# Output product and second norm of a hybrid block written in one fixed order: six token tiles begun, two finished by pairs of w_out's rows

## The chip, the cores and the metric

One core of a Trainium2 chip runs the whole kernel. The metric is the device time of one execution in microseconds. TensorE is the matmul engine, VectorE, ScalarE and GpSimd are the elementwise engines (DVE, ACT and POOL in the rows), and SyncE (SP) issues nearly all DMAs from one queue, in order.

## The reference

One layer: a bidirectional RG-LRU block over 256 context and 1024 latent tokens, then a gated ConvFFN over the latent tokens. D_MODEL is 1024, LRU_WIDTH 1280, FFN_HIDDEN 2816, batch 1, fp32. What matters for the change is the end of the mixer and the norm behind it:

```python
out = lambda y, r: (jax.nn.gelu(y) * r.astype(y.dtype)) @ w_out      # r: both scans, added
x = x + gate1 * out(y_lat, r_lat)                                    # only the latent tokens are kept
h2 = rms_norm(x) * (1.0 + scale2) + shift2                           # second norm, feeds the ConvFFN
u = h2 @ w_up                                                        # then conv 3x3, silu(a) * v, w_down
```

(The last three lines are the layer's wiring in short; rms_norm divides by the root of the mean square of 1024 channels.)

## The kernel before

Every fp32 product is made of three matmuls on a rounded "high" part and the "low" rest: high x high, low x high, high x low (`mm`, line 87). The high part is a cast on ScalarE, the low part a subtraction (`lo_part`, line 84) on VectorE or GpSimd. So each operand of a product costs one cast and one subtraction of its size before TensorE can read it.

The scans run channels on partitions: ten blocks t of 128 channels, each 1280 tokens wide. Block t's result, scan forward plus scan backward times gelu(y), goes to DRAM: blocks 0 to 7 to `rgd`, block 8 to `rgd8`, block 9 to `rgd9`. The output product runs tokens on partitions: eight token tiles i of 128, two halves c of 512 output columns, ten blocks k. For one tile and half that is 30 matmuls of 128x512. The tile's operand is read back from `rgd` as an 8x128 slab (`rgr`), split into `rgh` and `rgl`. In the first half, blocks 8 and 9 come from SBUF (`r8h/l`, `r9h/l`), in the second from DRAM (`rg2`). w_out comes in pairs m of row blocks (2m, 2m+1) for one half: `wo_pair(pool, c, m)` loads 512 KB (`wor`), casts (`woh`) and subtracts (`wol`). There are two raw buffers for these pairs, shared with all other weights (tag `raw`), and five split ones.

The first half is begun while the last block's scans run (lines 638 to 697). `first(i)` does blocks 0 to 7 of tile i into a bank of PSUM; five tiles are begun (five banks of `ps_b`), then block 8 is added to the five, then block 9. This part is written under a manual schedule: TensorE, VectorE, ScalarE and GpSimd execute it in the order of the text. From line 700 on there is no manual schedule; a scheduler orders the instructions from the loop over c and i. It does tiles 5 to 7 of the first half whole, then the second half in banks `ps_d` (two, used in turn). For each tile, `pb` is multiplied by the gate g1 and added to x1 (lines 744 and 745). In the second half x1[i] is then complete, and the norm follows at once: square and sum, Sqrt, reciprocal and a Newton step (`rstd_of`), scale and shift into `xn`, eight transposes on TensorE into `pt` (two banks of `ps_t`), cast and subtraction into `h2h` and `h2l`. The first two up-projection tiles take tokens 0 to 511 before the last tile's norm, and tokens 512 to 1023 after it. The rest of the ConvFFN, the same in both kernels, follows.

Of the kernel before, what the change touches and what calls it, by code (L numbers as in the profile page):

```python
# [19 lines left out]
P = 128  # L20
# [45 lines left out]
def tile_kernel(ctx: ExitStack, tc: tile.TileContext, x, cx, par, mod_b, mod1, mod2, wyx, gw, w_out, w_up, w_down, fw, out):  # L66
# [52 lines left out]
    def rstd_of(n, srcs, junks, between=lambda: None):  # L119
# [7 lines left out]
        return [rs[:, i:i + 1] for i in range(m)]  # L127

# [371 lines left out]
    def rg_part(i, c):  # L500
        gh = op.tile([P, NCH, P], F32R, tag="rgh", name="rgh", bufs=2)
        gl = op.tile([P, NCH, P], F32R, tag="rgl", name="rgl", bufs=2)
        raw = op.tile([P, NCH - 2, P], F32, tag="rgr", name="rgr")
        cols = slice(i * P, (i + 1) * P)
        load(raw, rgd[:, :, cols].rearrange("t p n -> p t n"))
        S.copy(gh[:, :NCH - 2], raw)
        lo_part(V, gl[:, :NCH - 2], raw, gh[:, :NCH - 2])
        if c:
            r2 = op.tile([P, 2, P], F32, tag="rg2", name="rg2", bufs=2)
            for j in range(2):  # L510
                load(r2[:, j], rgd2[j][:, cols])
            S.copy(gh[:, NCH - 2:], r2)
            lo_part(V, gl[:, NCH - 2:], r2, gh[:, NCH - 2:])
        return gh, gl

    def out_mm(pb, c, i, rgs, ks):
        for k in ks:
# [3 lines left out]
            else:  # L521
                gh, gl = (r[:, k] for r in rgs)
# [26 lines left out]
    with tc.manual_schedule(engines={ENG.PE, ENG.DVE, ENG.Activation, ENG.Pool}):  # L549
# [102 lines left out]
        rgs = {0: rg0, 1: rg_load(op0, 1, 3), 2: rg_load(op0, 2, 3)}  # L652
        S.copy(rgs[1][0], rgs[1][2])
# [7 lines left out]
        def first(i):  # L661
            pbs[i] = bank()
            out_mm(pbs[i], 0, i, rgs[i][:2], range(NCH - 2))
# [3 lines left out]
        a_t = [decay(t, d, r_t[d]) for d in range(2)]  # L667
# [15 lines left out]
        lo_part(V, rgs[4][1], rgs[4][2], rgs[4][0])
        first(4)
        lo_part(V, last2[NCH - 2][1], hs8, last2[NCH - 2][0])
        wo_pair(op, 0, 4, V)
        recur(1, a_t[1], r_t[1], b_t[1])
        for i in range(5):
            out_mm(pbs[i], 0, i, None, (NCH - 2,))
# [4 lines left out]
        S.copy(last2[NCH - 1][0], hs)  # L694
        lo_part(V, last2[NCH - 1][1], hs, last2[NCH - 1][0])
        for i in range(5):
            out_mm(pbs[i], 0, i, None, (NCH - 1,))


    ps_x.release()  # L700
    wo_pair(wp, 1, 0)
# [24 lines left out]
    for c in range(2):  # L726
# [9 lines left out]
        for i in range(KD):  # L736
# [9 lines left out]
            if c == 0:  # L746
                continue
# [234 lines left out]
```

## Time and profile before

| | us |
|---|---|
| median of 3 runs | 1267.95 (1265.47 to 1268.74) |
| profiled execution | 1267.6 |
| its span, first to last instruction | 1265.8 |
| TensorE busy, VectorE busy | 1219.2, 1028.0 |
| ScalarE busy, GpSimd busy | 547.3, 398.9 |

The span divides into a head with the modulation, the blocks of the mixer with their scans up to about 389 us, the output product and second norm up to about 550 us, and the ConvFFN from there. A busy TensorE is not one at its peak: matmuls overlap, a 128x512 one is listed with 0.39 us and starts every 0.23 us. In the profile's rows the brackets give the idle time of an engine ahead of an instruction and what ended it.

### The profile page before, as it was taken

Reading aid. Unit: us, or ns where it says so; the run is one execution under the profiler, and the core shown is the slowest. Engines: PE = TensorE matmul, PEld = TensorE weight load, DVE = VectorE, ACT = ScalarE, POOL = GpSimd, SP = SyncE. Lnnn points to the kernel's source line nnn. Section 1 sums busy time; section 2 is a strip of 40 time slices with the busy share of each in tenths; the row PEclk is TensorE's granted clock in tenths of the full one; section 3 lists DMA queues with packets and bytes.
Section 4 is the critical chain, followed back from the end, with each engine's and each line's share of the span. In section 5 each row is a group of like instructions: output and inputs, shape, how many; then the busy total and the mean of one; then the engine's idle time right before and its main releaser. Section 6 shows DMA issues by size and latency. Waiting matters only on the chain.

```text
span 1265.8 us, 14253 instructions
## 1 busy us (share of the span) xinstructions
PE 1219.2 (96%) x5512; PEld 1001.2 (79%) x5512; DVE 1028.0 (81%) x1156; ACT 547.3 (43%) x691; POOL 398.9 (32%) x221
## 2 busy tenths in 40 slices
PE   7879999999999889999999999999999999999996
PEld 6768888888887668788888888888888888888875
DVE  6968999999978758679878777777777778777777
ACT  6468888888888134333212222222222112222244
POOL 4732222222220010252333333333333333334460
PEclk8789999999999999999999999999999999999999
DMA  8522333333325552221111111111111111111003
GB/s 321 179 69 98 125 125 126 125 125 125 109 67 154 199 178 85 67 79 40 49 50 50 51 50 50 50 50 37 41 41 50 50 51 50 50 50 50 17 1 133
DMA packets 55588, 108.21 MB, mean 85 GB/s; under 512 B 4440, under 2 KB 22872, under 8 KB 55520
## 3 DMA queue, kind: packets, MB, share of 16 engines
q1 hardware_dynamic: 55376, 107.04, 25.4%
q8 instruction: 43, 0.70, 0.2%
q10 hardware_dynamic: 144, 0.26, 0.1%
q14 instruction: 25, 0.20, 0.1%
HBM read 97.85 MB, written 9.44 MB: 85 GB/s over the span
## 4 chain that ended last, share of the span: by engine, by line
PE 83%; DVE 9%; ACT 3%; DMA 2%; issue 2%; POOL 1%; SPq 0%; ACTq 0%; DVEq 0%; POOLq 0%
PE u L87 37%; PE pd L87 21%; PE pb L87 14%; PE xp L87 10%; DVE hl L214 2%; DVE acc L803 1%; DVE o L922 1%; DVE md L215 1%; DMA wor<-w_out_dram 1%; DMA ld<-x_dram 1%; DVE rgl L84 1%; DVE x L836 1%; DMA rgr<-rgd 0%; PE pt L763 0%; PE pb L271 0%
## 5 line engine op out<-in xcount | busy, mean ns | idle before, releaser
L803 DVE SCALAR_TENSOR_TENSOR acc<-u,pr,acc 128x945 f32<-128x945 f32 (+2 forms) x352 | 427.1, 1219 | 24.7 <-ACT acc L796 17.3
L87 PE MATMUL u<-h2l,wh 128*128 128x512 f32 x704 | 276.6, 393 | 0.0
L87 PE MATMUL u<-h2h,wh 128*128 128x512 f32 x704 | 276.0, 392 | 0.2 <-ACT h2h L766 0.2
L87 PE MATMUL u<-h2h,wl 128*128 128x512 f32 x704 | 274.3, 390 | 0.0
L84 POOL TENSOR_TENSOR wl<-raw,wh 128x1024 fp32r<-128x1024 f32 x66 | 164.4, 2491 | 270.4 <-ACT wh L151 252.6
L836 DVE TENSOR_TENSOR x<-pd,x 128x512 f32<-128x512 f32 x160 | 109.2, 686 | 125.7 <-PE pd L87 125.7
L87 PEld LDWEIGHTS u<-h2h,wh 128*128 128x128 f32 x704 | 132.3, 188 | 29.9 <-ACT h2h L766 0.5
L87 PEld LDWEIGHTS u<-h2h,wl 128*128 128x128 f32 x704 | 132.7, 188 | 29.0
L87 PEld LDWEIGHTS u<-h2l,wh 128*128 128x128 f32 x704 | 132.6, 188 | 28.9 <-DVE h2l L84 0.4
L87 PE MATMUL pd<-dl,gh 128*128 128x512 f32 x320 | 126.4, 395 | 0.0
L87 PE MATMUL pd<-dh,gh 128*128 128x512 f32 x320 | 125.7, 393 | 0.8 <-ACT dt L833 0.8
L87 PE MATMUL pd<-dh,gl 128*128 128x512 f32 x320 | 124.4, 389 | 0.0
L882 ACT CAST gh<-acc 128x1024 fp32r<-128x1024 f32 x22 | 23.2, 1053 | 223.5 <-DVE acc L879 223.5
L84 POOL TENSOR_TENSOR gl<-acc,gh 128x1024 fp32r<-128x1024 f32 x18 | 43.3, 2408 | 198.8 <-ACT gh L882 198.8
L878 ACT ACTIVATE acc<-acc 128x1024 f32<-128x1024 f32 x22 | 23.3, 1060 | 182.8 <-DVE acc L803 182.8
L151 ACT CAST wh<-raw 128x1024 fp32r<-128x1024 f32 x64 | 67.2, 1050 | 75.7 <-PE u L87 69.9
L87 PE MATMUL xp<-hh,wh 128*128 128x512 f32 (+1 forms) x240 | 85.6, 369 | 2.0 <-ACT hh L224 2.0
L87 PE MATMUL xp<-hl,wh 128*128 128x512 f32 (+1 forms) x240 | 81.3, 364 | 4.0 <-POOL hl L84 4.0
L87 PEld LDWEIGHTS pd<-dh,gh 128*128 128x128 f32 x320 | 60.0, 187 | 14.0 <-ACT dt L833 1.2
L87 PEld LDWEIGHTS pd<-dl,gh 128*128 128x128 f32 x320 | 60.0, 187 | 13.9
L87 PEld LDWEIGHTS pd<-dh,gl 128*128 128x128 f32 x320 | 60.2, 188 | 13.4
L815 POOL TENSOR_TENSOR dr<-dr,g 128x512 f32<-128x512 f32 x40 | 51.5, 1306 | 57.9 <-DMA dr<-w_down_dram 57.9
(205 smaller groups left out, 2229.9 us busy)
## 6 DMA issues: line engine op xcount, KB each, us to landing
raw<-w_up_dram SPq DMA_DIRECT2D x44, 512.0 KB, 3.4
mraw<-mod_dram SPq DMA_DIRECT2D x64, 256.0 KB, 4.1
raw<-wyx_dram SPq DMA_DIRECT2D x20, 512.0 KB, 3.6
dr<-w_down_dram SPq DMA_DIRECT2D x40, 256.0 KB, 4.7
ld<-mod_dram SPq DMA_DIRECT2D x16, 512.0 KB, 5.2
rgr<-rgd SPq DMA_DIRECT2D x16, 512.0 KB, 5.1
rgd<-r SPq DMA_DIRECT2D x10, 512.0 KB, 3.2
wor<-w_out_dram SPq DMA_DIRECT2D x10, 512.0 KB, 4.9
```

Source lines behind the costliest of these rows:

```text
L84: eng.tensor_tensor(lo, src, hi.bitcast(F32), op=ALU.subtract)
L87: T.matmul(o, w, r, start=start, stop=stop)
L151: S.copy(wh, raw)
L214: V.scalar_tensor_tensor(hl[KD - 1][:, :D], mr[k][s], 1.0, row, op0=ALU.mult, op1=ALU.mult, accum_out=md1[:, k, s, v:v + 1])
L215: V.tensor_scalar(md1[:, k, s], md1[:, k, s], mod_b1(k, s), None, op0=ALU.add)
L803: V.scalar_tensor_tensor(o, uv[:, r0 + dy:r1 + dy, c0 + dx:c1 + dx], w(dy, dx), o, op0=ALU.mult, op1=ALU.add)
L815: G.tensor_tensor(raw, raw, g2[:, cs], op=ALU.mult)
L836: V.tensor_tensor(xs, pd, xs, op=ALU.add)
L878: ordered(act(aa, aa, AF.Silu))
L882: S.copy(gh, aa)
L922: V.scalar_tensor_tensor(o, x1[i], rs, fwb, op0=ALU.mult, op1=ALU.mult)
```

## The change

The manual schedule now reaches to the end of the first two up-projection tiles, so the order of the four engines is that of the text (SyncE's is still the scheduler's).

First half: the eight banks of PSUM hold more tiles, since `ps_x` (three banks) is released early. Six tiles are begun with blocks 0 to 7. Loads are issued apart from the splits (`wo_load`, `wo_split`; `rg_load` one or two tiles ahead). The decays of the last block write to the memory of `xh` and `xl` and stand ahead of the previous block's sum. Block 9's split is done in halves of 512 tokens. Tiles 6 and 7 follow together, one pair of w_out's rows after the other, and behind each pair the buffers are refilled with the same pair of the second half. The gate and the add into x1 stand between these passes.

Second half: a tile's slab is loaded and split two tiles ahead (`rg_all`, `rg_split`); a tile's transposes stand two tiles behind its product, those of the last two among the up matmuls. The root is an estimate on ScalarE (Abs_reciprocal_sqrt) and a Newton step, in place of Sqrt, reciprocal and Newton. The low parts of w_out's last pairs and of the first two up weights are all on VectorE.

```diff
+    def rstd_est(ss, nv, rs, src, junk):
+        if src is not None:
+            act(junk, src, AF.Square, accum_out=ss, scale=D ** -0.5)
+        ordered(act(rs, ss, AF.Abs_reciprocal_sqrt, bias=eps))
+        act(nv, ss, AF.Identity, bias=meps, scale=-0.5)
...
+        ps_x.release()
+        ps_f = pool("ps_f", bufs=3, side="right", space=PSUM)
...
-        wo_pair(wp, 0, 2, V)
-        wo_pair(op, 0, 3, V)
+        wo_load(0, 2)
+        wo_load(0, 3)
...
+        lo_part(V, rgs[1][1], rgs[1][2], rgs[1][0])
+        rgs[3] = rg_load(op0, 3, 3)
         recur_scan(1, prev[1][1], prev[3][1])
-        lo_part(V, rgs[1][1], rgs[1][2], rgs[1][0])
+        lo_part(V, rgs[2][1], rgs[2][2], rgs[2][0])
+        rgs[4] = rg_load(op, 4, 2)
+        wo_load(1, 0)
+
+        a_t = [wk.tile([P, NTOK], F32, tag=tag, name="a") for tag in ("xh", "xl")]
+        for d in range(2):
+            decay_a(t, d, r_t[d], a_t[d])
+            decay_b(t, d, r_t[d])
...
+            pbs[i] = ps_f.tile([P, 512], F32, tag="pb", name="pb") if i in (2, 3, 4) else bank()
...
+        first(5)
+        recur_scan(1, a_t[1], b_t[1])
+        for i in range(6):
+            out_mm(pbs[i], 0, i, (NCH - 2,))
...
+        for q in range(2):
+            cols = slice(q * 512, (q + 1) * 512)
+            S.copy(last2[NCH - 1][0][:, cols], hs[:, cols])
+            lo_part(V, last2[NCH - 1][1][:, cols], hs[:, cols], last2[NCH - 1][0][:, cols])
+        for i in range(6):
+            out_mm(pbs[i], 0, i, (NCH - 1,))
...
+        for m in range(5):
+
+            for i in (6, 7):
+                out_mm(pbs[i], 0, i, (2 * m, 2 * m + 1))
+            wo_split(wp if m < 3 else op, 1, m, V)
+            if m < 3:
+                wo_load(1, m + 2)
+            if m == 0:
+                to_gated(4)
...
+            elif m == 1:
+                rg_split(0)
+                rg_all(1)
+                to_x1(4)
+                to_x1(5)
+            elif m == 3:
+                rg_split(1)
+        for i in (6, 7):
+            to_gated(i)
+            to_x1(i)
...
+        cs = slice(512, D)
+        for i in range(KD):
+            if i + 2 < KD:
+                rg_all(i + 2)
+            pbs[i] = ps_d.tile([P, 512], F32, tag="pd", name="pd")
+            out_mm(pbs[i], 1, i, range(2))
+            if i > 1:
+                turn(i - 2)
+                h2_part(i - 2, True)
+            out_mm(pbs[i], 1, i, range(2, NCH))
+            if i > 1:
+                h2_part(i - 2, False)
+            to_gated(i)
+            to_x1(i)
+            if i + 2 < KD:
+                rg_split(i + 2)
+            if i == KD - 1:
+                wu[tiles[1]] = split(raw, V)
+            xns[i] = op1.tile([P, D], F32, tag="xn", name="xn", bufs=2)
+            ss, nv, rs, tm = (stat[:, j, 10 + i:11 + i] for j in range(4))
+            rstd_est(ss, nv, rs, x1[i], xns[i])
+            rstd_step(nv, rs, tm)
...
+        for k in range(3):
+            up_k(0, us[0], 0, k)
+        turn(KD - 2)
...
+        for k in range(KD // 2):
+            up_k(1, us[1], 0, k)
+        turn(KD - 1)
```

`turn(i)` is the eight transposes of tile i, `h2_part` its casts (True) or its subtractions (False), `to_gated` and `to_x1` the gate and the add.

The first place where the order is read is VectorE around the last block's scans. Before (r_3289 is the last block's result, a_3399 its backward scan, rgl the low parts of token tiles, r9rgl that of block 9):

```order
L84 TENSOR_TENSOR wol_3505<-wor_3502,woh_3504 128x1024
L459 SCALAR_TENSOR_TENSOR r_3289<-a_3399,r_3289 128x1280
L84 TENSOR_TENSOR rgl_3589<-rgr_3590,rgh_3588 128x1024
L460 TENSOR_TENSOR b_3307<-b_3307,r_3289 128x1280
L467 SCALAR_TENSOR_TENSOR a_3399<-a_3399,b_3307 128x256
L468 SCALAR_TENSOR_TENSOR a_3399<-a_3399,b_3307 128x1024
L473 TENSOR_TENSOR r_3289<-a_3396,a_3399 128x1024
L477 TENSOR_TENSOR r_3289<-r_3289,gy_3236 128x1024
L84 TENSOR_TENSOR rgl_3629<-rgr_3630,rgh_3628 128x1024
L84 TENSOR_TENSOR r9rgl_3531<-r_3289,r9rgh_3530 128x1024
```

After (a_3361 is that scan, rgl_3489 and rgl_3520 are tiles 6 and 7):

```order
L84 TENSOR_TENSOR rgl_3452<-rgr_3453,rgh_3451 128x1024
L470 SCALAR_TENSOR_TENSOR r_3289<-a_3361,r_3289 128x1280
L471 TENSOR_TENSOR b_3307<-b_3307,r_3289 128x1280
L84 TENSOR_TENSOR r8l_3456<-r_3056,r8h_3455 128x1024
L84 TENSOR_TENSOR wol_3527<-wor_3342,woh_3526 128x1024
L478 SCALAR_TENSOR_TENSOR a_3361<-a_3361,b_3307 128x256
L479 SCALAR_TENSOR_TENSOR a_3361<-a_3361,b_3307 128x1024
L484 TENSOR_TENSOR r_3289<-a_3360,a_3361 128x1024
L488 TENSOR_TENSOR r_3289<-r_3289,gy_3236 128x1024
L84 TENSOR_TENSOR r9rgl_3583<-r_3289,r9rgh_3582 128x512 x2
L84 TENSOR_TENSOR rgl_3489<-rgr_3490,rgh_3488 128x1024
L84 TENSOR_TENSOR rgl_3520<-rgr_3521,rgh_3519 128x1024
```

One tile's subtraction has moved from among the scan's steps to ahead of them, the one between the result and block 9's low part to behind it, and block 9's is two instructions of 512.

The second place is VectorE at the end of the first half. Before (wol are w_out's last pairs, pb_3667 is tile 7 of the first half, pd_3755 tile 0 of the second):

```order
L84 TENSOR_TENSOR wol_3713<-wor_3710,woh_3712 128x1024
L84 TENSOR_TENSOR rgl_3824<-rgr_3825,rgh_3823 128x1024
L744 TENSOR_TENSOR pb_3667<-pb_3667,g1_82 128x512
L84 TENSOR_TENSOR wol_3719<-wor_3716,woh_3718 128x1024
L745 TENSOR_TENSOR x1_7_3570<-pb_3667,x1_7_3570 128x512
L84 TENSOR_TENSOR wol_3725<-wor_3722,woh_3724 128x1024
L84 TENSOR_TENSOR rgl_3824<-rg2_3829,rgh_3823 128x256
L84 TENSOR_TENSOR wol_3731<-wor_3728,woh_3730 128x1024
L744 TENSOR_TENSOR pd_3755<-pd_3755,g1_82 128x512
L745 TENSOR_TENSOR x1_0_3563<-pd_3755,x1_0_3563 128x512
```

After (wol_3749 is the last pair, pb_3643 and pb_3644 are tiles 6 and 7, wl is the first up weight, pd_3791 tile 0 of the second half):

```order
L84 TENSOR_TENSOR wol_3711<-wor_3661,woh_3710 128x1024
L84 TENSOR_TENSOR wol_3729<-wor_3683,woh_3728 128x1024
L84 TENSOR_TENSOR rgl_3690<-rgr_3691,rgh_3689 128x1024
L84 TENSOR_TENSOR rgl_3690<-rg2_3692,rgh_3689 128x256
L84 TENSOR_TENSOR wol_3749<-wor_3714,woh_3748 128x1024
L755 TENSOR_TENSOR pb_3643<-pb_3643,g1_82 128x512
L758 TENSOR_TENSOR x1_6_3620<-pb_3643,x1_6_3620 128x512
L755 TENSOR_TENSOR pb_3644<-pb_3644,g1_82 128x512
L758 TENSOR_TENSOR x1_7_3621<-pb_3644,x1_7_3621 128x512
L84 TENSOR_TENSOR wl_3763<-raw_3760,wh_3762 128x1024
L755 TENSOR_TENSOR pd_3791<-pd_3791,g1_82 128x512
L758 TENSOR_TENSOR x1_0_3614<-pd_3791,x1_0_3614 128x512
```

The last three pairs stood among and behind tile 7's gate and add; now gate and add of tiles 6 and 7 stand behind the last pair, and the first up weight's subtraction stands between them and the second half's first tile.

## Rows read from the trace of the kernel before

**Rows 1.** The page: chain that ended last, shares of the span by engine.

```profile
PE 83%; DVE 9%; ACT 3%; DMA 2%; issue 2%; POOL 1%; SPq 0%; ACTq 0%; DVEq 0%; POOLq 0%
```

**Rows 2.** Windows, 376 to 550 us: length, busy time (x instructions), granted clock, DMA.

```profile
390.00:400.00 10.00, 7.57 (x33) 5.70 (x32) 9.35 (x9) 6.43 (x7) 0.00 (x0) 1.00 0.43 142
...
420.00:430.00 10.00, 5.86 (x21) 4.28 (x20) 8.39 (x7) 2.10 (x2) 0.00 (x0) 0.88 0.50 153
...
460.00:470.00 10.00, 7.64 (x24) 5.17 (x25) 5.03 (x7) 4.16 (x6) 2.39 (x1) 0.83 0.56 174
...
520.00:530.00 10.00, 8.03 (x34) 6.30 (x33) 9.19 (x14) 2.41 (x5) 2.26 (x1) 0.83 0.63 202
```

**Rows 3.** Waits of TensorE, 376 to 600 us: us, times, longest.

```profile
PE pb L87 <- ACT r9rgh L694: 3.4, 1, 3.4
PE pb L87 <- DVE rgl L84: 2.4, 1, 2.4
PE pd L87 <- ACT woh L488: 2.4, 2, 1.9
PE pt L763 <- DVE xn L758: 2.0, 1, 2.0
PE pb L87 <- DVE x L745: 1.4, 1, 1.4
```

**Rows 4.** Timeline, TensorE: start us, us, engine, line, operation, out<-in, xcount.

```profile
389.00 0.40 PE L87 MATMUL pb<-woh,rgh 128*128 128x512 f32 x1
...
398.03 0.40 PE L87 MATMUL pb<-woh,rgh 128*128 128x512 f32 x1
...
419.43 0.39 PE L87 MATMUL pb<-wol,rgh 128*128 128x512 f32 x1
...
427.85 0.80 PE L87 MATMUL pb<-woh,r9rgl 128*128 128x512 f32 x1 [0.77 <-DVE r9rgl L84]
```

**Rows 5.** Chain of waits by time, 378 to 600 us: start, us, what.

```profile
453.15 4.32 DMA wor<-w_out_dram
...
459.82 3.65 DMA wor<-w_out_dram
...
474.74 0.87 PE pt L763 x8
...
539.00 46.80 PE u L87 x204
```

**Rows 6.** Windows, 550 us to the end (columns as in rows 2).

```profile
550.00:600.00 50.00, 50.00 (x221) 41.27 (x221) 47.94 (x43) 16.51 (x16) 16.70 (x9) 1.00 0.18 62
```

**Rows 7.** Lines by form, VectorE, 389 to 530 us: xcount, busy, mean, idle.

```profile
L84 DVE TENSOR_TENSOR rgl<-rgr,rgh 128x1024 fp32r<-128x1024 f32 x15 | 18.3, 1221 | 7.6 <-ACT rgh L506 7.5
...
L84 DVE TENSOR_TENSOR h2l<-pt,h2h 128x512 fp32r<-128x512 f32 x14 | 9.0, 684 | 2.6 <-ACT h2h L766 2.5
...
L744 DVE TENSOR_TENSOR pd<-pd,g 128x512 f32<-128x512 f32 x8 | 5.6, 695 | 2.3 <-PE pd L87 2.2
...
L468 DVE TENSOR_TENSOR_SCAN a<-a,b 128x1024 f32<-128x1024 f32 x2 | 4.7, 2352 | 0.1
```

**Rows 8.** Timeline, ScalarE; in brackets the idle time before, and releaser.

```profile
398.58 1.37 ACT L442 ACTIVATE a<-r,sp 128x1280 f32<-128x1280 f32 x1 [3.52 <-DVE r L473]
...
404.02 1.28 ACT L669 ACT_TABLE_LOAD   x1
405.31 2.44 ACT L669 ACTIVATE r<-r 128x1280 f32<-128x1280 f32 x2
```

**Rows 9.** Waits of VectorE, 376 to 540 us.

```profile
DVE r L459 <- ACT r L669: 2.3, 1, 2.3
```

**Rows 10.** Tile rgr, 370 to 530 us: last line of its answer.

```profile
DMA to landing us min/median/max: 4.2/4.8/5.3
```

**Rows 11.** Lines by form, ScalarE, 389 to 530 us (columns as in rows 7).

```profile
L488 ACT CAST woh<-wor 128x1024 fp32r<-128x1024 f32 x8 | 8.3, 1048 | 7.7 <-DMA wor<-w_out_dram 6.2 <-PE pb L87 1.6
```

**Rows 12.** Tile x, 370 to 470 us: the loads of x1.

```profile
DMA to landing us min/median/max: 10.8/10.8/10.8
```

More of the change, by code (lines that the diff above doesn't have):

```diff
@@ L521, in out_mm @@
             else:
-                gh, gl = (r[:, k] for r in rgs)
+                gh, gl = (r[:, k] for r in rgs[i][:2])
             mm(pb, gh, wh[:, k % 2], k == 0, False)
@@ L693, in tile_kernel @@
         last2[NCH - 1] = [op0.tile([P, LAT], F32R, tag=n, name=f"r9{n}", bufs=3) for n in ("rgh", "rgl")]
[L694 to L701, printed above, removed]
-    opa.release()
-    wk.release()
-    gwp.release()
-    x1p = pool("x1")
-    x1 = [x1p.tile([P, D], F32, name=f"x1_{i}") for i in range(KD)]
-    def weight_up(n):
-        raw = wp.tile([P, KD, P], F32, tag="raw", name="raw", bufs=2)
-        load(raw, w_up[n].rearrange("p (k m) -> p k m", k=KD))
-        return split(raw, G)
@@ new lines, in tile_kernel @@
+        for q in range(2):
[5 more added lines that the diff above has]
+        for i in (6, 7):
+            lo_part(V, rgs[i][1], rgs[i][2], rgs[i][0])
+        opa.release()
+        wk.release()
+        gwp.release()
+        x1p = pool("x1")
+        x1 = [x1p.tile([P, D], F32, name=f"x1_{i}") for i in range(KD)]
@@ new lines, in x1_load, with to_gated, to_x1 @@
+        def x1_load(i):
+            load(x1[i], x[i * P:(i + 1) * P])
+        def to_gated(i):
+            V.tensor_tensor(pbs[i], pbs[i], g1[:, cs], op=ALU.mult)
+        def to_x1(i):
+            V.tensor_tensor(x1[i][:, cs], pbs[i], x1[i][:, cs], op=ALU.add)
+        cs = slice(0, 512)
+        for i in range(4):
+            x1_load(i)
+        rg_all(0)
+        for i in range(4, KD):
+            x1_load(i)
+        for i in range(3):
+            to_gated(i)
+        to_x1(0)
+        to_gated(3)
@@ new lines, in tile_kernel, with up_load, weight_up, up_psum @@
+        for i in (6, 7):
+            to_gated(i)
+            to_x1(i)
+        op0.release()
+        op1 = pool("op1", side="right")
+        tiles = [n for j in range(NF) for n in (j, NF + j)]
+        wu = {}
+        us = {}
+        def up_load(n):
+            raw = wp.tile([P, KD, P], F32, tag="raw", name="raw", bufs=2)
+            load(raw, w_up[n].rearrange("p (k m) -> p k m", k=KD))
+            return raw
+        def weight_up(n):
+            return split(up_load(n), G)
+        def up_psum(pos):
+            return (ps_u2 if pos % 3 == 2 else ps_u).tile([P, LAT], F32, tag="u", name="u")
@@ new lines, in tile_kernel, with turn @@
+        raw = up_load(tiles[1])
+        ps_f.release()
+        ps_b.release()
+        ps_d = pool("ps_d", bufs=2, space=PSUM)
+        ps_u = pool("ps_u", bufs=2, space=PSUM)
+        ps_t = pool("ps_t", bufs=2, side="right", space=PSUM)
+        h2p = pool("h2")
+        h2h = h2p.tile([P, KD, LAT], F32R, name="h2h")
+        h2l = h2p.tile([P, KD, LAT], F32R, name="h2l")
+        xns, pts = {}, {}
+        def turn(i):
+            pts[i] = [ps_t.tile([P, 512], F32, tag="pt", name="pt") for q in range(2)]
+            for k in range(KD):
+                T.transpose(pts[i][k // 4][:, k % 4 * P:(k % 4 + 1) * P], xns[i][:, k * P:(k + 1) * P], ident)
```

172 lines of the change are left out of this document (80 added, 92 removed).

## The prediction

> **What bounds the kernel now.** I read the chain of waits first: TensorE holds 83% of it [rows 1]. So only those stretches can give time where TensorE stands still or runs at a lower clock. The windows show where: 420 to 430 us has a granted clock of 0.88, 460 to 470 and 520 to 530 have 0.83, and 390 to 400 has TensorE busy only 7.57 of 10 us at full clock [rows 2]. All lie in the output product and second norm, which is what is changed. The waits of TensorE name the causes: 3.4 us for the high part of the last channel block (r9), 2.4 for the low part of token tile 1, 2.4 for w_out's high part, 2.0 for the normed tile xn, 1.4 for x1 [rows 3].
>
> How much is lost there in all? The product's matmuls start at 389.00 us. Those from 398.03 to 419.43 are 92 intervals: 0.2326 us each [rows 4]. The work up to the end of the first two up-projection tiles is fixed: 480 product matmuls x 0.2326 = 111.6 us, eight sets of transposes x 0.87 = 7.0, and 96 up matmuls x 0.2294 (46.80 us for 204) = 22.0 [rows 5]: 140.6 us. The last 48 of these start at 539.00 [rows 5] and end at 539.00 + 48 x 0.2294 = 550.0. So 161.0 us pass for 140.6 of work: **20.4 us are lost**, 11.6 of them in the five waits shown, about 10 x (0.12 + 0.17 + 0.17) = 4.6 by the clock, the rest in short gaps. After 550 us TensorE is busy without a break (50.00 of the first 50) [rows 6].
>
> **The change part by part.**
> *First half, tiles 0 to 5.* The wait of 2.4 for tile 1's low part goes: its subtraction now stands ahead of two scans, of which the longer alone takes 2.35 [rows 7], so it ends about 3 us earlier, more than the wait was long; TensorE asks at 389.0 + 25 x 0.2326 = 394.8. Exp no longer takes the memory of the previous block's a tiles, for which it idled 3.52 us [rows 8]; it takes that of xh and xl, which the gate matmuls have left by 389. So Sqrt ends some 3.5 us earlier, and the 2.3 us for which VectorE stood before the last r go [rows 9]. For r9: VectorE did the same five tile subtractions before it; now it is 2.3 us earlier, one subtraction of 1.22 [rows 7] stands behind r9's, and r9 is split into halves (0.6 less). TensorE had the first low part at 427.85 [rows 4]; now 427.8 - 2.3 - 1.2 - 0.6 = 423.7, and 1 to 2 us more where dependent steps have no cover between them: up to 425.6. TensorE has a sixth tile in front: 389.0 + 144 x 0.2326 + 18 x 0.23 = 426.6. The wait is gone with 1.0 to 2.9 us to spare. Tile loads: each needs the buffer of the tile two before it; loads land in 4.2 to 5.3 us [rows 10]. Tile 5's is late next: its buffer is free when tile 3's subtraction ends, about 404.3, and SP has the rgd8 store and the first rg2 read (which waits for that store) ahead of it; issued at 404.8 it lands by 410.1, is cast in 1.05 [rows 11] and is in time for the subtraction at about 411.2.
>
> *Tiles 6 and 7.* Both have free banks and parts, so the wait for x1 goes. 60 matmuls: 430.7 to 444.8 (= 389.0 + 240 x 0.2326, no wait). The two passes share the w_out pair m, and after each pass its buffers are split anew for the second half. This is the place of my first cost. Pair (1,0) can be cast at 433.5 and is subtracted by 435.9; only then may load (1,2) go (two raw buffers), landing after 3.65 to 4.32 us as its like did [rows 5], about 440.2. Behind tile 0's casts and subtractions and two x1 adds VectorE reaches (1,2) at 442.5 and ends at 443.7; load (1,4) goes at 443.8 and lands at 448.1; cast and subtraction: 450.4. TensorE wants its low part at 444.8 + 26 x 0.2326 = 450.9. No wait, but nothing to spare. The eight x1 loads, 10.8 us to landing before [rows 12], are ahead of them in the queue: issued from about 424.4, right behind block 9's store, and done by about 438.
>
> *Second half.* VectorE's queue has gate and add of tiles 6 and 7 behind the subtraction of pair (1,4): 450.4 + 4 x 0.695 = 453.2 [rows 7]. As the program is built, the first pd tile lies in the bank of tile 1, long free, but the second in the bank of tile 7. TensorE reaches the second at 444.8 + 30 x 0.2326 = 451.8 and waits: 453.2 - 451.8 = 1.4, with the handing over **1.5** (bounds: 0.8 if the load lands after 3.65 us, 2.4 if after 5.3). Such a wait (1.9, 2.0) was followed by a mean clock of 0.83 in its 10 us; the one of 2.4 was not [rows 2, 3]. Bounds 0 and 1.7; I take 1.7. Then the first transposes: the normed tile 0 needs gate and add 1.4, square and root about 1.9 (a pass of ScalarE like the cast's 1.05 [rows 11], and small steps), one table load 1.28 [rows 8], Newton about 0.4, xn two passes like the subtractions' 1.22: about 0.3 us later than TensorE asks: 0.3.
>
> From there a tile takes TensorE 30 x 0.2326 + 0.87 = 7.85 us. VectorE has three passes of 1.22, 2 x 0.684 and 2 x 0.695 = 6.4 [rows 7], about 0.9 of small ones, and waits about 0.5 for the root: just inside. The transposes, now two tiles later, ask 9.2 us after the product, xn is there after 6.2: the 2.0 us wait for xn goes. Tile 7's is asked for 36 up matmuls after its product (8.3 + 0.9) and ready after 8. The root itself (two small VectorE instructions fewer per tile) lies beside TensorE: nothing. Up weights on VectorE instead of GpSimd: wl of tile 0 is in the chain above, that of tile 1 falls in the last tile's slack.
>
> A rule speaks against the root's new table. The Trainium skill (ScalarE: Activation LUTs, "What ACT_TABLE_LOAD costs") counts 1.28 us plus a drain of about 1.38 for every switch. The trace here has 1.28, and the next instruction starts at 405.31, 1.29 us after the load began [rows 8]; no drain shows. By the rule the first transposes would wait 1.7, not 0.3 us, and the sum would be 1.4 us higher.
>
> *Sum:* -20.4 + 1.5 + 1.7 + 0.3 = **-16.9 us**. The profiled execution took 1267.6, 0.35 below the median of 1267.95: 1267.6 - 16.9 + 0.35 = **1251.0 us**.
>
> **The rivals.**
> *No new wait* (0.20): loads land early enough or the wait for tile 7's bank is short and leaves the clock. For it: 3.65 is a landing seen. Against: VectorE's order itself puts four instructions behind the last split. -20.4: 1247.5.
> *w_out's loads stay late* (0.22): the second half starts with the waits of before (2.4 for woh, the subtraction, 1.7 of clock: about 4.5) on top of mine, because x1 and tile loads crowd the queue. For it: before, x1 took 10.8 us. Against: here x1 starts earlier. 1255.5; with one wait more, 1259.
> *The up-projection eats it* (0.03): VectorE is busy 47.94 of 50 us from 550 to 600 [rows 6]; if it sets the pace there, TensorE's earlier start becomes a wait. Against: VectorE's start moves with it, and TensorE waits for nothing there. 1268.
> *Slower* (0.04): the tile load as the second half's clock. One raw buffer: load, cast 1.05, subtraction 1.22, then the next load. With 4.8 us to landing [rows 10] that is 7.2, below 7.85. With x1's 10.8 it is 13.2: six tiles x 5.4 = 32 us, less the gain: 1283. It decides from a landing of 5.4, and breaks even at 5.4 + 16.9/6 = 8.2. Against: no x1 load is in flight then.
>
> **How the numbers follow.** My forecast has 0.51, its own range is 1248.5 to 1253.5. The range for 8 in 10 takes in the case without waits and the late loads: 1246.5 to 1259. A measurement here can tell about 0.3%, 3.8 us, from no change: faster means below 1264.1. Faster: 0.51 + 0.20 + 0.22 = 0.93; same 0.03; slower 0.04.
>
> **What would show it.** In the waits of TensorE the rows for r9rgh, rgl, woh, xn and x should be gone or under 0.5 us, and one row pd <- DVE x (the add of tile 7) of 1 to 2 us should be new, near 452 us. The first up matmul should stand near 509, not 522. A clock of 1.00 in every window but the one at 450 to 460. I am wrong if TensorE waits for tiles' parts (rgl) again, if waits for w_out's low parts exceed 2 us, or if the stretch from 389 us to the end of the second up tile is not 142 to 148 us long.

## The result and the profile after

Before 1267.58 us (median of 4 runs), after **1248.53 us** (1246.67 to 1250.26, 4 runs): ratio 0.985, 95% interval 0.983 to 0.987. The forecast was 1251.0.

| | before | after |
|---|---|---|
| profiled execution, us | 1267.6 | 1246.7 |
| its span, us | 1265.8 | 1244.8 |
| first matmul of the product, us | 389.00 | 387.95 |
| **stage**: from there to the end of the second up-projection tile, us | 161.0 | **141.15** |

The span is 21.0 us shorter. 19.9 of them lie in the stage that the change rewrites; 1.05 lie ahead of it, in a part that is the same in both. In some executions that part takes about 10 us more, so rows of different runs stand up to 11.5 us apart, and the experiments are compared by the stage's length rather than by times of day. The stage is worked out as in the prediction: after, the last transposes start at 514.68, 126.73 us after the first product matmul, and 60 up matmuls follow them; for every run below it is that distance plus the same 14.42.

The chain that ended last, by engine, answers to [rows 1]:

```profile
PE 86%; DVE 8%; ACT 3%; DMA 1%; issue 1%; POOL 0%; SPq 0%; ACTq 0%; DVEq 0%
```

The windows, with the columns of [rows 2]:

```profile
390.00:400.00 10.00, 10.00 (x44) 7.95 (x43) 9.93 (x9) 9.89 (x9) 0.00 (x0) 1.00 0.58 185
...
420.00:430.00 10.00, 10.00 (x46) 8.25 (x45) 9.19 (x12) 1.14 (x2) 0.00 (x0) 1.00 0.71 260
...
450.00:460.00 10.00, 9.20 (x40) 7.00 (x39) 8.28 (x12) 4.92 (x8) 0.00 (x0) 1.00 0.66 214
460.00:470.00 10.00, 10.00 (x52) 8.37 (x52) 9.41 (x14) 6.20 (x15) 0.00 (x0) 1.00 0.23 68
```

All waits of TensorE from 376 to 600 us, answering to [rows 3]:

```profile
PE pd L87 <- DVE x L758: 0.8, 1, 0.8
PE pb L87 <- DVE b L449: 0.3, 1, 0.3
```

All five waits of before are gone, TensorE is busy 10.00 of 10 where it had 7.57 and 5.86, and no window from 380 to 550 us has a granted clock under 1.00. (The granted clock is a mean over the window: 1.00 is the higher of the clock's two levels, 2.4 GHz, and 0.83 says that TensorE ran part of the 10 us at the lower one, 1.2 GHz.) The row of 0.3 lies ahead of the product and was there before. The one new wait is the one foretold, for the bank of tile 7, one of the first half's last two tiles. TensorE's timeline at that place:

```profile
450.19 0.39 PE L87 MATMUL pd<-wol,rgh 128*128 128x512 f32 x1
451.38 0.50 PE L87 MATMUL pd<-woh,rgh 128*128 128x512 f32 x1 [0.80 <-DVE x L758]
```

From start to start 1.19 instead of 0.23: 0.96 us lost. VectorE there (start, duration, in brackets the idle time before and its releaser):

```profile
445.37 1.23 DVE L84 TENSOR_TENSOR rgl<-rgr,rgh 128x1024 fp32r<-128x1024 f32 x1 [0.96 <-ACT rgh L532]
...
447.43 1.23 DVE L84 TENSOR_TENSOR wol<-wor,woh 128x1024 fp32r<-128x1024 f32 x1 [0.50 <-ACT woh L502]
448.57 0.69 DVE L755 TENSOR_TENSOR pb<-pb,g 128x512 f32<-128x512 f32 x1
...
450.63 0.69 DVE L758 TENSOR_TENSOR x<-pb,x 128x512 f32<-128x512 f32 x1
```

ScalarE casts the pair in front of the second of these rows, when its load has landed:

```profile
446.35 1.05 ACT L502 CAST woh<-wor 128x1024 fp32r<-128x1024 f32 x1 [0.71 <-DMA wor<-w_out_dram]
```

This is the chain that the prediction counted: load, cast, subtraction of w_out's last pair, four instructions. What it did not count is the row ahead of it: VectorE stands 0.96 us for the second half's token tile 1 (rgr, cast to rgh), and that counts in the experiments. In this execution it costs nothing, since the subtraction behind it still waits 0.50 for its own cast.

The chain of waits behind it, in order of time (start, duration, what), answers to [rows 5]:

```profile
438.30 3.72 DMA wor<-w_out_dram
...
451.38 8.61 PE pd L87 x36
459.98 0.96 PE pt L839 x8
...
505.61 2.10 PE u L87 x9
...
514.84 0.87 PE pt L839 x8
```

From 451 us on it is TensorE alone. The first transposes take 0.96 instead of 0.87.

### The profile page after: what moved, and what is told of

Its sections match the earlier page's. It is cut to its first block, busy times and chain, and to the rows that moved or that the text cites. A ratio compares the mean times of both kernels' runs of the same rounds, so it can differ in the third digit from the quotient of the medians.

```text
span 1244.8 us, 14237 instructions
## 1 busy us (share of the span) xinstructions
PE 1212.7 (97%) x5512; PEld 999.0 (80%) x5512; DVE 1027.9 (83%) x1144; ACT 550.6 (44%) x701; POOL 388.7 (31%) x218
## 4 chain that ended last, share of the span: by engine, by line
PE 86%; DVE 8%; ACT 3%; DMA 1%; issue 1%; POOL 0%; SPq 0%; ACTq 0%; DVEq 0%
PE u L87 38%; PE pd L87 21%; PE pb L87 17%; PE xp L87 10%; DVE hl L225 3%; DVE acc L920 1%; DVE md L226 1%; DVE o L1034 1%; PE pt L839 1%; DMA ld<-x_dram 1%; DVE x L953 1%; PE pb L282 0%; DVE xc L417 0%; DMA raw<-w_up_dram 0%; DMA wor<-w_out_dram 0%
## 5 line engine op out<-in xcount | busy, mean ns | idle before, releaser
L84 POOL TENSOR_TENSOR wl<-raw,wh 128x1024 fp32r<-128x1024 f32 x64 | 159.1, 2486 | 340.7 <-ACT wh L162 332.8
```

Source lines behind the costliest of these rows:

```text
L84: eng.tensor_tensor(lo, src, hi.bitcast(F32), op=ALU.subtract)
```

## The experiments

Each run is the changed kernel with one edit (one run undoes two parts together, the last adds its edit to another run's); times are medians, the stage is that of the one profiled execution, ratios are against the kernel before, which ran on the same chip. Their intervals are 0.5 to 0.9% wide, so two runs that differ by a few us are told apart by the stage and its waits. The diffs are cut; `...` marks where.

| run | time, us | ratio (95%) | stage, us | against 141.15 |
|---|---|---|---|---|
| five tiles begun | 1254.46 | 0.991 (0.988 to 0.993) | 147.5 | +6.35 |
| tiles 6, 7 whole | 1256.26 | 0.992 (0.989 to 0.995) | 148.4 | +7.3 |
| root as before | 1249.11 | 0.987 (0.984 to 0.990) | 141.6 | +0.4 |
| transposes one tile behind | 1255.84 | 0.993 (0.990 to 0.995) | 144.2 | +3.0 |
| tile 7's gate and add earlier | 1248.85 | 0.984 (0.981 to 0.988) | 142.0 | +0.8 |
| tile 1's low part late | 1253.65 | 0.989 (0.985 to 0.993) | 144.1 | +2.95 |
| one pass more | 1252.14 | 0.989 (0.986 to 0.993) | 144.45 | +3.3 |
| two passes more | 1253.28 | 0.989 (0.986 to 0.993) | 145.4 | +4.3 |
| gate, add, then tile 1 | 1248.94 | 0.984 (0.981 to 0.987) | 141.1 | 0.0 |
| a's memory and r9 as before | 1254.88 | 0.990 (0.986 to 0.993) | 146.7 | +5.6 |
| low parts on GpSimd | 1251.99 | 0.988 (0.984 to 0.992) | 143.35 | +2.2 |
| earlier table load | 1248.52 | 0.986 (0.982 to 0.991) | 140.0 | -1.15 |

**Five tiles begun.**

```diff
-        first(5)
         recur_scan(1, a_t[1], b_t[1])
-        for i in range(6):
+        for i in range(5):
             out_mm(pbs[i], 0, i, (NCH - 2,))
...
-        for i in range(6):
+        for i in range(5):
             out_mm(pbs[i], 0, i, (NCH - 1,))
+        first(5)
+        out_mm(pbs[5], 0, 5, (NCH - 2, NCH - 1))
```

> The changed kernel with five tiles begun instead of six: tile 5 is computed whole behind the last block's (r9) matmuls of tiles 0 to 4; all orders of VectorE and ScalarE stay. Yardstick here and in the runs that follow: the stage from the first matmul of the product to the end of the second up-projection tile, 161.0 us before, 141.15 in the changed kernel. Theory A (a sixth tile covers the wait for r9): TensorE asks for r9 at 387.95 + 135 x 0.2326 = 419.4 us, the first high part is cast at about 422.1, the low part ends at 423.4: a wait of 2.7 and one of about 1, then a lower clock as behind the 3.4 of before, about 1.4: stage 146.3 (145 to 147.5), total +5 us on the changed kernel. Theory B (VectorE's earlier r alone removed it; the sixth tile is spare): under 1 us of wait, stage 141 to 142.

TensorE's timeline and the window around it:

```profile
422.83 0.49 PE L87 MATMUL pb<-woh,r9rgh 128*128 128x512 f32 x1 [2.97 <-ACT r9rgh L736]
```

```profile
420.00:430.00 10.00, 6.94 (x22) 5.32 (x23) 9.19 (x12) 1.14 (x2) 0.00 (x0) 0.83 0.72 258
```

Theory A: the sixth tile covers a wait of 3 us and a fall of the clock behind it. It was 6.35 instead of the 5.15 expected. About 0.6 of the difference is the wait for tile 7's bank, 1.4 here instead of 0.8; the rest was not followed up.

**Tiles 6 and 7 whole.**

```diff
+        out_mm(pbs[6], 0, 6, range(NCH))
         for m in range(5):
-            for i in (6, 7):
-                out_mm(pbs[i], 0, i, (2 * m, 2 * m + 1))
+            out_mm(pbs[7], 0, 7, (2 * m, 2 * m + 1))
```

> The changed kernel with tile 6 computed whole and then tile 7, instead of pair by pair of w_out's rows; the splits of the second half's w_out pairs follow tile 7's passes. Theory A (taking both tiles through each pair frees w_out's buffers about 5.6 us earlier, and that pays): pair (1,0) is cast at 438 instead of 432.4, the load of pair (1,4) goes at about 448.6 and lands at 452.5 where TensorE wants it at 451: waits for rgl or woh of about 2, for woh/wol (1,4) of about 3.5, for tile 7's bank of about 2 instead of 0.8: stage 148 (146 to 150), total +7. Theory B (loads have spare time): stage within 1 us of 141.15.

Its waits of TensorE, 384 to 600 us:

```profile
PE pd L87 <- ACT woh L502: 1.5, 2, 1.4
PE pd L87 <- DVE rgl L84: 1.1, 1, 1.1
PE pd L87 <- DVE wol L84: 1.0, 2, 0.5
PE pd L87 <- DVE x L758: 0.6, 1, 0.6
```

Theory A: pair (1,0) is cast 5.5 us later than in the changed kernel, counted from the product's first matmul. 4.2 us of waits follow from 445 to 459 us, and the clock falls to 0.78 and 0.88 in two windows. Only 2.5 of the 4.2 are w_out's parts; 1.1 is a token tile's low part, which stands behind w_out's subtractions on VectorE, and 0.6 is tile 7's bank.

**The root as before.**

```diff
-            rstd_est(ss, nv, rs, x1[i], xns[i])
-            rstd_step(nv, rs, tm)
+            rs, = rstd_of(10 + i, [x1[i]], [xns[i]])
```

> The changed kernel with the second norm's root as before: Square, Sqrt, reciprocal and Newton step (two small VectorE instructions more per tile, about 0.14 + 0.17 us). Theory A (the root lies beside TensorE): xn of tile 0 about 0.3 us later, a wait of at most 0.4 for it, stage 141.2 to 141.7, total 0. Theory B (VectorE is at the end of its slack, 0.27 to 0.47 us a tile): 0.3 us on each of 7 tiles, stage 143, total +2.

The only wait is tile 7's bank, 1.3 us; none for xn. The 0.4 us are that wait, which varies between executions (0.8 to 1.5 over these runs). Theory A.

**Transposes one tile behind.**

```diff
-            out_mm(pbs[i], 1, i, range(2))
-            if i > 1:
-                turn(i - 2)
-                h2_part(i - 2, True)
-            out_mm(pbs[i], 1, i, range(2, NCH))
+            out_mm(pbs[i], 1, i, range(NCH))
+            if i:
+                turn(i - 1)
+                h2_part(i - 1, True)
...
+            if i:
+                h2_part(i - 1, False)
...
-        turn(KD - 2)
```

> The changed kernel with each tile's transposes one tile behind its product (behind the next tile's whole product) instead of two; low parts of h2 behind gate and add. Theory A (the two tiles of distance cover the norm): TensorE asks for xn of tile 0 at 451.38 + 30 x 0.2326 = 458.4, it is there at 459.8: a wait of 1.4; later tiles: ready about 1.4 + 1.3 + 1.6 + 0.4 + 2.5 = 7.2 us after the product plus ScalarE's steps, asked 7.0 after: 0.3 to 0.7 each on six tiles; stage 145 (143.5 to 147), total +4. Theory B (a tile is paced by TensorE's 7.85 us whatever the distance): only the first wait, stage 142 to 142.6.

```profile
PE pt L839 <- DVE xn L872: 1.9, 2, 1.3
PE pd L87 <- DVE x L758: 1.5, 1, 1.5
```

Neither theory in full: the first transposes wait 1.3 as both said, of the others only the last tile's, 0.7, where theory A had six such waits. The stage, 144.2, lies in theory A's range, but 0.7 of its 3.0 is the longer wait for tile 7's bank. The last tile's wait is not one of distance alone: a 128 x 1 instruction of its root took 2.09 us on VectorE beside a GpSimd subtraction, 0.22 in the other seven tiles (more on this under *Root, VectorE's pace, up weights*). The clock is 1.00 in every window, behind a wait of 1.5 (to 452.7 us) and one of 1.3 (to 461.1). The profiled execution, 1250.28, is the fastest of eight and 5.6 us below their median, so the usual price of this edit may be well above 3.0; no trace shows where it lies.

**Tile 7's gate and add ahead of w_out's last pair.**

```diff
+            if m == 4:
+                to_gated(7)
+                to_x1(7)
             wo_split(wp if m < 3 else op, 1, m, V)
...
-        for i in (6, 7):
-            to_gated(i)
-            to_x1(i)
+        to_gated(6)
+        to_x1(6)
```

> The changed kernel with gate and add of tile 7 moved ahead of the subtraction of w_out's last pair (1,4) on VectorE; tile 6's stay behind it. Theory A (the one wait that the change adds is set by VectorE's order): tile 7's bank is free at 446.9 + 1.4 = 448.3 us, TensorE asks at 450.4; the subtraction starts 0.9 later, at 448.3, and ends at 449.5, before TensorE asks: no wait for the bank, stage 140.2 (140 to 140.5), total -0.9. Theory B (w_out's last pair is the real limit): the wait moves to wol, 0.5 to 1 us, stage 141.

VectorE's timeline, then TensorE's waits:

```profile
449.59 1.23 DVE L84 TENSOR_TENSOR rgl<-rgr,rgh 128x1024 fp32r<-128x1024 f32 x1 [2.30 <-ACT rgh L532]
...
452.40 1.22 DVE L84 TENSOR_TENSOR wol<-wor,woh 128x1024 fp32r<-128x1024 f32 x1
```

```profile
PE pd L87 <- DVE wol L84: 1.2, 1, 1.2
PE pt L841 <- DVE xn L875: 0.2, 1, 0.2
```

Theory A falls in this execution: the wait moves to wol, as theory B said, and the stage is 1 us longer than theory B's 141. VectorE stood 2.30 us for the token tile's load, came to gate and add only at 451.07, and so to the subtraction 1.1 us after its cast was done (451.29): that is the wait for wol. The cast of that load began 57.75 us after the product's first matmul, 56.34 in the changed kernel's profile. With the earlier landing the subtraction would have ended 1.4 us sooner, by estimate ahead of TensorE's request, so the run shows that the place depends on this load, not that it can never pay.

**Tile 1's low part behind the scan.**

```diff
-        lo_part(V, rgs[1][1], rgs[1][2], rgs[1][0])
-        rgs[3] = rg_load(op0, 3, 3)
         recur_scan(1, prev[1][1], prev[3][1])
+        lo_part(V, rgs[1][1], rgs[1][2], rgs[1][0])
+        rgs[3] = rg_load(op0, 3, 3)
```

> The changed kernel with the subtraction of token tile 1 behind the backward scan again. Theory A (its place ahead of the scans removed a wait of 2.4 that nothing gives back): rgl is there at 393.28 + 3.1 = 396.4, TensorE asks at 387.95 + 25 x 0.2326 = 393.8: a wait of 2.5, stage 143.7 (143 to 144.5), total +2.5, clock 1.00 (behind the 2.4 of before it was 1.00). Theory B (VectorE's own work sets the later stage, so an early wait is given back): stage 141 to 142.

The wait (it ends at 407.87 us in this run) and its window:

```profile
PE pb L87 <- DVE rgl L84: 2.4, 1, 2.4
```

```profile
400.00:410.00 10.00, 7.58 (x33) 5.71 (x32) 9.39 (x8) 9.90 (x10) 0.00 (x0) 1.00 0.39 130
```

Theory A: the wait of [rows 3] is back to the tenth, nothing returns it, and the clock stays at 1.00.

**One and two passes more** ahead of tile 7's gate (one shown).

```diff
+        xd = op1.tile([P, D], F32, tag="xn", name="xn", bufs=2)
+        V.tensor_tensor(xd, sh2, sc2, op=ALU.mult)
         for i in (6, 7):
             to_gated(i)
             to_x1(i)
...
```

The memory pool of `xn` is opened ahead of the loop for it, instead of behind.

> The changed kernel with one more VectorE pass over 128 x 1024 (its result is not used) ahead of gate and add of tiles 6 and 7: the wait for tile 7's bank grows by 1.2, from 0.8-1.5 to 2.0-2.7 us. Theory A (the prediction's: behind a wait of about 2 us the clock stands at 0.83 in its 10 us): stage 141.15 + 1.2 + 1.7 = 144 (143.7 to 144.5). Theory B (one wait of this size leaves the clock; behind the 2.4 for rgl it stayed at 1.00, and the 0.83 at 460 us stood behind five waits that sum to 4 us): clock 1.00, stage 142.3 to 143.

> As the run before it with two such passes: the wait for tile 7's bank becomes 3.2 to 3.9 us. Theory A: clock 0.83 in the 10 us, stage 141.15 + 2.4 + 1.7 = 145.3. Theory B (a longer single wait does lower it, as the 3.4 for r9 before and the 3.0 with five tiles did, both 0.83 to 0.88): the same 145.0 to 145.5 here; the two part in the run with one pass. Theory C (a wait at this place never lowers it): clock 1.00, stage 143.5 to 144.

TensorE with one pass more, its window, and TensorE with two:

```profile
463.44 0.64 PE L87 MATMUL pd<-woh,rgh 128*128 128x512 f32 x1 [2.61 <-DVE x L758]
```

```profile
460.00:470.00 10.00, 7.39 (x26) 5.57 (x25) 8.29 (x13) 4.32 (x8) 0.00 (x0) 0.83 0.64 200
```

```profile
456.20 0.67 PE L87 MATMUL pd<-woh,rgh 128*128 128x512 f32 x1 [3.64 <-DVE x L758]
```

Theory A holds for the sizes that it named: behind 2.61 us eight matmuls start 0.43 apart instead of 0.23, which is 1.6 us; the stage lost 1.5 beside the longer wait. So the prediction's price of a fall (1.7) was about right; what was wrong is that a wait of 1.5 was given it. A single wait left the clock at 1.00 at 0.8, 1.3, 1.5 and 2.4 us, and had 0.83 behind it at 2.6, 3.0 and 3.6. Length alone does not decide, though: at 2.0 us both are on record. The wait for xn before the change, the only one listed between 466 and 539 us, was followed by 0.83, and the 2.0 in the run with low parts on GpSimd by 1.00. No run shows what told these two apart.

**Gate and add of tile 7, then tile 1's subtractions, then w_out's pair.**

```diff
+            if m == 4:
+                to_gated(7)
+                to_x1(7)
+                rg_split(1)
             wo_split(wp if m < 3 else op, 1, m, V)
...
-            elif m == 3:
-                rg_split(1)
-        for i in (6, 7):
-            to_gated(i)
-            to_x1(i)
+        to_gated(6)
+        to_x1(6)
```

> The changed kernel with gate and add of tile 7 and then the two subtractions of token tile 1's second-half load put ahead of the subtraction of w_out's pair (1,4) on VectorE. In the run with tile 7's gate and add alone moved, VectorE had stood 2.30 us for that token tile's load (rgr) before it reached them, and the wait went to wol (1.2). Theory A (the limit is the landing of that load; gate and add of tile 7 fit into VectorE's wait for it): the bank is free 58 us after the product's first matmul, asked for at 62.4; pair (1,4) ends at 61.4, asked for at 61.6: waits of 0 to 0.3 in all, stage 140.2 to 140.5, total -0.8 on the changed kernel. Theory B (whatever stands behind that load waits): wol or rgl 0.8 to 1.3, stage 141 to 142.

```profile
PE pt L840 <- DVE xn L874: 0.9, 1, 0.9
```

The wait for the bank is gone, as theory A said, and the stage is as long as before: the same 0.9 us are now waited for the norm of tile 0, which neither theory had. In the changed kernel, delayed by the bank's wait, TensorE had come to the transposes just when xn was there. The norm came no earlier because ScalarE casts token tile 2's load ahead of tile 0's square, and that cast began 64.6 us after the product's first matmul here, 64.5 in the changed kernel.

**The last block's a tiles and r9 as before.**

```diff
-        a_t = [wk.tile([P, NTOK], F32, tag=tag, name="a") for tag in ("xh", "xl")]
+        a_t = [wk.tile([P, NTOK], F32, tag="a", name="a", bufs=2) for d in range(2)]
...
-        for q in range(2):
-            cols = slice(q * 512, (q + 1) * 512)
-            S.copy(last2[NCH - 1][0][:, cols], hs[:, cols])
-            lo_part(V, last2[NCH - 1][1][:, cols], hs[:, cols], last2[NCH - 1][0][:, cols])
+        S.copy(last2[NCH - 1][0], hs)
+        lo_part(V, last2[NCH - 1][1], hs, last2[NCH - 1][0])
```

> The changed kernel with two parts undone: the last block's a tiles take the memory of the block before again (so Exp waits for that block's last use of it), and r9's parts are made in one piece, not in halves. Theory A (both only widened a margin that the sixth tile already gives: r9's low part ended at 423.4 us, TensorE asked at 426.0): r9 is 2.3 + 0.6 later, a wait of 0.3 (0 to 0.8), stage 141.2 to 142. Theory B (r9 stays what TensorE waits for, these parts paid most of the 3.4): a wait over 1.5, stage 143 and more.

ScalarE, VectorE and TensorE in this run:

```profile
400.70 1.37 ACT L453 ACTIVATE a<-r,sp 128x1280 f32<-128x1280 f32 x1 [4.66 <-DVE r L484]
```

```profile
408.74 1.49 DVE L470 SCALAR_TENSOR_TENSOR r<-a,r 128x1280 f32<-128x1280 f32 x1 [3.42 <-ACT r L703]
...
414.53 2.33 DVE L84 TENSOR_TENSOR rgl<-rgr,rgh 128x1024 fp32r<-128x1024 f32 x2
```

```profile
415.79 0.72 PE L87 MATMUL pb<-woh,rgl 128*128 128x512 f32 x1 [3.03 <-DVE rgl L84]
```

Both theories looked at r9, and TensorE did not wait for it. Exp waited 4.66 us for the memory, VectorE 3.42 for its root, and what was late is tile 4's low part, which stands behind that work on VectorE: 3.0 us, with the fall of the clock behind it (0.83 in 410 to 420). The two parts were undone together; the rows put the wait on the chain that starts at the memory, so the memory of the a tiles is one of the change's large parts, and its price is not at r9. What r9 would cost by itself stays open: TensorE came to it 42.4 us after the product's first matmul instead of 37.6, and its low part, done by 40.0, was there.

**Low parts of the first up weights on GpSimd.**

```diff
-        lo_part(V, wu[tiles[0]][1], raw, wu[tiles[0]][0])
+        lo_part(G, wu[tiles[0]][1], raw, wu[tiles[0]][0])
...
-                wu[tiles[1]] = split(raw, V)
+                wu[tiles[1]] = split(raw, G)
```

> The changed kernel with the low parts of the first two up-projection weights made on GpSimd, as before, instead of VectorE. Theory A (on VectorE they stand beside TensorE's work): stage as without, 141 to 142, total 0; xn of tile 0 is there 1.2 us earlier, which nobody waits for. Theory B (the 1.2 on VectorE between gate and add of tile 7 and the first norm counts): stage shorter by 0.5 to 1.2. Theory C (GpSimd's subtraction slows VectorE's passes beside it): passes longer than 1.22, stage longer by up to 1.

TensorE's wait, then ScalarE, VectorE and GpSimd around it:

```profile
PE pt L839 <- DVE h2l L84: 2.0, 1, 2.0
```

```profile
519.95 1.05 ACT L162 CAST wh<-raw 128x1024 fp32r<-128x1024 f32 x1 [1.60 <-DMA raw<-w_up_dram]
520.90 0.29 ACT L133 ACTIVATE stat<-stat,eps 128x1 f32<-128x1 f32 x1
```

```profile
521.41 2.08 DVE L137 SCALAR_TENSOR_TENSOR stat<-stat 128x1 f32<-128x1 f32 x1 [4.25 <-ACT stat L134]
```

```profile
521.07 2.40 POOL L84 TENSOR_TENSOR wl<-raw,wh 128x1024 fp32r<-128x1024 f32 x1 [2.41 <-ACT wh L162]
```

None of the three theories as stated: the wait stands at the other end of the stage, where the low part that frees the transposes' bank comes behind tile 7's norm on VectorE. The stage is 2.2 us longer, 2.4 with the transposes behind the wait, which take 0.2 longer too. In this program the third weight's cast, which waits for its load, stands ahead of the root on ScalarE; and VectorE's first small instruction of the root, 0.22 us elsewhere, takes 2.08 and ends at 523.49, when GpSimd's subtraction (521.07 to 523.47) does. The granted clock behind this wait of 2.0 is 1.00:

```profile
520.00:530.00 10.00, 8.01 (x39) 6.22 (x38) 7.24 (x8) 3.51 (x7) 4.08 (x3) 1.00 0.58 206
```

**The table loaded early**, added to the run with gate, add and tile 1's subtractions:

```diff
+        ordered(act(stat[:, 2, 25:26], eps, AF.Abs_reciprocal_sqrt))
         for i in range(KD):
```

> The run with tile 7's gate and add ahead of token tile 1's subtractions, and besides the table of the estimated reciprocal root loaded early: one such instruction on a 128 x 1 tile, whose result is not used, on ScalarE ahead of the second half. In that run the wait for tile 7's bank (0.8 to 1.5) was gone, but the first transposes waited 0.9 for xn of tile 0, whose chain holds the table load of 1.28 us, so the stage stayed at 141.1. Theory A (these two waits stood one behind the other, nothing else is late): xn of tile 0 is there 1.28 earlier, no wait for xn or the bank, stage 140.2 (140.0 to 140.5): the floor of 140.6 that the prediction worked out, within its rounding. Theory B (a third chain, the landing of token tile 2's load on ScalarE ahead of the square, is as late): a wait of 0.5 to 0.9 stays, stage 141.

```profile
444.12 15.28 PE pd L87 x66
459.40 0.87 PE pt L840 x8
```

Theory A: in the chain of waits, 66 matmuls (two tiles and six of the third) run without a gap into the first transposes, and TensorE waits for nothing in the stage. So 140.0 is what the stage takes without a wait. In the whole kernel the 1.15 us do not show: 1248.52 against 1248.53, far inside the intervals.

## Why the prediction was right, step by step

*The lost time* (20.4 of 161.0): 19.9 came back, and a version without any wait has 140.0, so 21.0 were there; the floor of 140.6 was 0.6 too high.

*First half.* Tile 1's low part: confirmed at its size, 2.4 of wait. The sixth tile: confirmed, 3.0 of wait and the clock without it. r9: foretold there at 423.7 to 425.6, which is 422.65 to 424.55 with the earlier start (1.05); its first low part is made from 422.81 and done in about 0.65, inside that, and TensorE asks for it at 425.76. The memory for Exp: that it matters is right, the place is not. The prediction spent its 2.3 us on r9 alone; the run shows that without it tile 4's low part comes 3.0 us late. It had listed tile 5's load as late next and never put tile 4's subtraction against its request. In the changed kernel that subtraction starts 21.1 us after the product's first matmul, in the run 24.5.

*Tiles 6 and 7.* Confirmed: pair by pair is worth 7.3 us. The times that the prediction worked out hold when the earlier start (1.05) is taken off: pair (1,0) was foretold cast at 433.5 and was at 432.44; pair (1,4) subtracted from about 449.2 and was from 447.43, 0.7 better.

*The wait for tile 7's bank* (1.5; bounds 0.8 and 2.4): the place was right, the lost time 0.96 in this execution, and the wait 1.3 and 1.5 in two others. So was the chain, but for tile 1's token load, which stands in front of it on VectorE and was left out: gate and add of tile 7 were free of w_out's pair only when they stood ahead of that load too. The size of the wait follows the cast of w_out's last pair, which begins when its load has landed: begun 58.4, 58.6, 58.9 and 59.2 us after the product's first matmul (the changed kernel, low parts on GpSimd, root as before, transposes one tile behind) it went with waits of 0.80, 0.93, 1.30 and 1.47. That bears out the chain, and the bounds that were set by the landing.

*The lower clock behind it* (1.7, bounds 0 and 1.7): **this is the term that was mis-sized**, 0 measured. Of the two waits that it was read from, the 1.9 [rows 3] was no model for a single one: it was one of four within 8 us, as TensorE's timeline of before has them:

```profile
458.59 0.50 PE L87 MATMUL pd<-woh,rgh 128*128 128x512 f32 x1 [0.52 <-ACT woh L488]
459.85 0.50 PE L87 MATMUL pd<-wol,rgh 128*128 128x512 f32 x1 [0.52 <-DVE wol L84]
...
464.65 0.50 PE L87 MATMUL pd<-woh,rgh 128*128 128x512 f32 x1 [1.85 <-ACT woh L488]
465.91 0.80 PE L87 MATMUL pd<-wol,rgh 128*128 128x512 f32 x1 [0.42 <-DVE wol L84]
```

The 2.0 did stand alone and was followed by 0.83; the 2.4 for tile 1's low part stood alone too, and behind it the clock was 1.00. So those two gave the bounds, 0 and 1.7, and no choice between them. The wait nearest in size, the 1.4 for x1 in [rows 3], had matmuls 0.23 apart behind it; that was the row to size the term by:

```profile
434.17 0.50 PE L87 MATMUL pb<-woh,rgh 128*128 128x512 f32 x1 [1.38 <-DVE x L745]
434.51 0.39 PE L87 MATMUL pb<-woh,rgl 128*128 128x512 f32 x1
434.74 0.40 PE L87 MATMUL pb<-wol,rgh 128*128 128x512 f32 x1
```

*First transposes* (0.3): 0.1. The table load has its 1.28 (454.99 us) and the next instruction starts 1.29 after it, at 456.28; the drain of 1.38 that the Trainium skill (ScalarE: Activation LUTs, "What ACT_TABLE_LOAD costs") adds to each switch does not show here either. Yet the term was closer to mattering than its size said: with the bank's wait gone, these transposes waited 0.9.

*Root, VectorE's pace, up weights* (0): confirmed for the root and for the pace of a tile (no wait from 452 to 600 us). The low parts are hidden on VectorE; on GpSimd they are not, 2.2 us. That move was worth more than the nothing it was given, and the trace of before had its row. VectorE's small instructions of tile 6's root, the GpSimd subtraction of an up weight beside them, and TensorE's wait for xn behind:

```profile
520.02 0.17 DVE L110 RECIPROCAL stat<-stat 128x1 f32<-128x1 f32 x1 [0.97 <-ACT stat L124]
520.22 2.06 DVE L113 SCALAR_TENSOR_TENSOR stat<-stat 128x1 f32<-128x1 f32 x1
519.87 2.39 POOL L84 TENSOR_TENSOR wl<-raw,wh 128x1024 fp32r<-128x1024 f32 x1 [0.54 <-ACT wh L151]
525.20 1.06 PE L763 MATMUL pt<-ident,xn 128*128 128x128 f32 x8 [1.97 <-DVE xn L758]
```

2.06 instead of the 0.22 of the other seven tiles, ending with GpSimd's subtraction (522.28 and 522.26): 1.84 of the 1.97 us that TensorE waited, by estimate. So the 2.0 for xn in [rows 3] was for the most part this delay, and not too short a distance of the transposes, by which the prediction explained it. By its own figures (asked for after 9.2, there after 6.2) the two tiles of distance leave 3.0 us and would have covered such a delay too; which of the two parts removed the wait is not separated. The runs with low parts on GpSimd and with transposes one tile behind each have one such instruction again, 2.08 and 2.09.

*The sum*: -16.9 foretold, -19.9 in the stage. Of the 3.0 between them 1.7 are the clock, 0.5 the bank, 0.2 the transposes and 0.6 the floor. Of the rivals, *no new wait* was nearest in time, 1247.5, though a wait was there; w_out's late loads, the up-projection and the tile load's pace did not appear. The prices of single parts do not add up to the gain: undone one at a time, the first half's three, the pairs, the distance and GpSimd cost 27 us together, where all of the change brought 19.9, so each holds only with the others in place. Not tried were the earlier loads of x1, the memory of the a tiles and r9's halves, each by itself.

*The number*: that 1248.53 lies in the forecast's own range, 1248.5 to 1253.5, is in part luck; it is 0.03 inside. Signs that the prediction had named for itself failed, all on the fast side: the stage is 141.15 where anything outside 142 to 148 was to mean that it is wrong, the new wait is 0.8 and not 1 to 2, the clock is 1.00 from 450 to 460 as well, and the first up matmul stands at 505.4, not near 509. The mechanism held: the waits that were to go went, and the one that was to come stands where it was foretold.

## What to carry to other kernels

Several near-critical chains may meet at one point: removing the wait that shows (the bank, 0.8) can give nothing until the one behind it (the norm, 0.9) is shortened too, so look for what the next instruction on the engine asks for before you move anything. What a wait costs beside its length is not told by its length alone: read the granted clock behind every wait on record, with the waits just before it, and where waits of like length differ, keep the term a range. Look for single instructions that take far longer than their like: one of 2.06 us among seven of 0.22 was the cause of a wait that looked like one of order. When a producer is made earlier, follow its engine's queue to every consumer behind it; the one that pays may not be the one whose wait the profile showed.

## What the runs showed of the hardware

A VectorE instruction on 128 x 1 with two inputs, usually 0.22 us, took 2.06, 2.08 and 2.09 us beside a GpSimd subtraction in three runs (before, low parts on GpSimd, transposes one tile behind), and both ended within 0.02 us of each other. A reciprocal on 128 x 1, with one input, kept its 0.17 beside such a subtraction (520.02 us before). The Trainium skill (SBUF — State Buffer, "SBUF: two separate sides") says that VectorE with two inputs in SBUF and GpSimd reading SBUF take a shared pair of ports as a lock, whole instruction by whole instruction; these rows agree. A single wait of 2.4 us left the granted clock at 1.00, one of 2.6 was followed by 0.83 in its 10 us, and of two of 2.0 one had 1.00 and one 0.83 behind it. The wait for tile 7's bank differed by 0.7 us between runs that leave its chain alone (0.8 after, 1.3 and 1.5 in two others), with the landing of one load.
